# The scan's second block gets a buffer of its own and is prepared among the value streams; the recurrent streams' weights are loaded by single feature tiles

## The chip, the cores and the metric

The kernel runs on one core of a Trainium2 chip. The metric is the device time of one execution in microseconds (us). Five engines work side by side, each through its own instructions in the order in which they are written into the program: PE (matrix products), DVE (vector), ACT (scalar and activation functions), POOL and SP (here mostly the issuer of DMA transfers). They meet through semaphores. An instruction that waits holds up everything behind it on its engine.

## What is computed

One layer of a bidirectional encoder on 1024 tokens of width 1024: a SwiGLU feed-forward block, a mixing layer, a second feed-forward block, each between RMS norms. The mixing layer projects the normed tokens once (`z = h @ w_in`), runs dilated attention on one part of the columns and a bidirectional RWKV-7 recurrence on the other, and projects both back. Of the recurrence this is what matters here:

```python
def _rwkv7_step(state, inp):
    r, w, k, v, kk, kka = inp
    sa = jnp.einsum('dbhvk,dbhk->dbhv', state, kk)
    state = state * w[..., None, :] - sa[..., :, None] * kka[..., None, :] + v[..., :, None] * k[..., None, :]
    y = jnp.einsum('dbhvk,dbhk->dbhv', state, r)
    return state, y
```

r, k and v are columns of z, each token mixed with its two neighbours; kk is k scaled and normalised by head; the decay w and the rate inside kka come from small products of z. There are eight heads of 64 features and two directions.

## The kernel before

**How the work is staged.** First feed-forward block, projection of the attention columns, attention; under the attention the engines already work at the recurrent streams; then the scan; then the output projection and the second feed-forward block. The change lies between the end of attention and the first quarter of the scan.

**The streams.** `project_rwkv` (L499) makes the twelve recurrent streams, one for each feature tile (`ct`) of 128 features: 4 to 7 are k, 0 to 3 are r, 8 to 11 are v (stream 0 is made elsewhere). Its argument is a list of (first tile, number of tiles) pairs. For each pair `columns` (L426) loads eight pieces of the weight, one for each 128 rows, into `zraw` (L431, four buffers) and splits each into a high part `zh` (ACT, L186) and a low part `zl` (DVE, L187); both have sixteen buffers, which is two pairs' worth. Each feature tile is then 48 matrix products of 512 tokens (L510): two halves of the tokens, eight pieces, three products. `shift` mixes in the neighbours (ACT L522 and L523, DVE L524 and L525), and `stream` stores the tile. A value tile is also reversed (DVE L605), turned by PE (L611), copied out by ACT (L613) and stored in token order (SP, L615); the scan reads it back later. I call the four value streams V8 to V11.

**The scan** walks over eight blocks of 128 tokens, each block in both directions. A block goes through four steps:

- `prep` (L783): for each direction, loads of decay, rate, r, k and kk (`in`, `th_w`, `th_a`), two exponentials, six DVE operations (L810, L811, L814, L815, L821, L822), 16 products `lp` (L830) whose results DVE masks into `lm` (L832, four times), and 16 transposes `bp` (L838). One direction is called a half-preparation below. At the end the diagonal pieces of `lm` go to memory (L846).
- `solve` (L850): loads those pieces as `X`, and inverts 32 by 32 triangles in 31 pairs of DVE operations (L866, L868), each of which needs the one before; a copy (L870) ends it; POOL stores the result (L872, L873).
- `merge` (L875): POOL loads the result back (L883, L886), PE makes the 64 by 64 inverses (`pa` L894, `pb` L900), ACT copies them (L896, L902).
- `chain` (L918): two chunks of 64 tokens after each other, each of them xu (L941), a copy `xs` (L944), xu again (L952), a copy `uv` (L954), the new state `st` and the output y (L937), and the state's product with the decay on DVE (L968, twice for a chunk). The next chunk starts from that.

What `prep` leaves of a block (`lm`, `pr`, `bt`, `gc`; 32 KB in each partition) lives until its chain has ended. Before the change block 0 has the buffer `R0`, which is taken from space beside the streams' tiles, and the other blocks have the two buffers of the pool `B0`, which lies where the normed tokens `x` were. So block 1's buffer is free only when the last value product has read x. Blocks 3 and 5 use `R0` again.

**What sets the order.** The program is written in the order of `run` (L1163), and a scheduler places every instruction on its engine by that order as a priority and by its own idea of when inputs are ready. `upto(m)` prepares and solves blocks up to m; `project_attended` (L1066) is the attention half of the output projection of 128 tokens (24 products of 512 columns, L1064, with weights `woh` and `wol` whose low part DVE makes at L1055); it is called twice after chain 0 and once after each later chain.

Of the kernel before, what the change touches and what calls it, by code (L numbers as in the profile page):

```python
# [10 lines left out]
F32 = mybir.dt.float32  # L11
# [152 lines left out]
class _Kernel:  # L164
# [998 lines left out]
    def run(self):  # L1163
        nc = self.nc
        R = dict(side="right")
# [3 lines left out]
        with self.top as top:  # L1169
# [5 lines left out]
            x = self.operand(xp, xp)  # L1175
            x0 = self.io["x"][0]

            with ExitStack() as st:
# [6 lines left out]
                f = self.factors(x, xt)  # L1185
# [50 lines left out]
                x = x2  # L1236
# [10 lines left out]
            s_mc, s_at, s_sc, s_ps = (ExitStack() for _ in range(4))  # L1247
# [11 lines left out]
            NB, s_sr, s_pr, s_zr, s_pm = NC_ // BLK, ExitStack(), ExitStack(), ExitStack(), ExitStack()  # L1259
            pm = self.pool(s_pm, "ps_m", 1, space=PSUM, **R)  # L1260
            pp = self.pool(s_pr, "ps_p", 3, space=PSUM, **R)
            sp = self.pool(s_sr, "prep", 1, **R)
            R0 = self.pool(s_sr, "blk0", 1, **R)
            self.scan_constants(sp)
            zr, pz = self.pool(s_zr, "zr", 2), self.pool(s_zr, "ps_r", 1, space=PSUM)
            self.project_rwkv(zr, pz, x, [(4, 2), (6, 2), (1, 1), (2, 2)])
            blk = {0: self.prep(0, sp, pp, R0)}
            self.solve(0, sp)
            self.project_rwkv(zr, pz, x, [(8, 2), (10, 2)])
            s_zr.close()  # L1270
            s_xn.close()
            B0 = self.pool(s_sc, "blks", 2)
            sc = self.pool(s_sc, "scan")
            self.scan_inverses(sc)
            sc.tile([128, 96], F32, name="edge")
            s_eo, s_pe = ExitStack(), ExitStack()
            eo = self.pool(s_eo, "eo")
            pc = self.pool(s_ps, "ps_c", 1, space=PSUM)
            pe = self.pool(s_pe, "ps_e", 1, space=PSUM)
            self.sv = {}  # L1280
            nxt = [1]

            def upto(m):
                while nxt[0] <= min(m, NB - 1):
                    n = nxt[0]
                    blk[n] = self.prep(n, sp, pp, R0 if n in (3, 5) else B0)
                    self.solve(n, sp)
                    nxt[0] += 1

            upto(1)  # L1290
            rs_a = self.rstd(eo, self.ss_a.rearrange("p a b -> p (a b)"), NT * H, 1.0 / HD, EPS)
            self.merge(0, blk[0], sc, pm)
            upto(2)
            WA = self.out_weights(eo, 0, self.aog)
            for n in range(NB):
                if n:
                    self.merge(n, blk[n], sc, pm)
                self.chain(n, blk.pop(n), sc, pc)
                upto(n + 3)
                for t in ([0, 1] if n == 0 else [n + 1] if n + 1 < NT else []):  # L1300
                    self.project_attended(eo, sc, pe, t, WA, rs_a)
# [5 lines left out]
            x = self.operand(xr, xr, n=4)  # L1307
# [29 lines left out]
            f = self.factors(f0, None)  # L1337
# [97 lines left out]
```

## Time and profile before

| | |
|---|---|
| three runs | 2389.86, 2390.91, 2396.3 us; median 2390.91 |
| the profiled execution | 2398.21 us |
| its span, first to last instruction | 2396.4 us |
| PE, DVE, ACT, POOL busy | 93%, 74%, 43%, 24% |
| mean granted PE clock | 0.951 |

Times in the profile are microseconds from the span's start. A row of the view by engine names start, duration, engine, line and operation, what is written from what, how many follow each other, and in brackets how long the engine had been idle before and which instruction ended the wait. DVE operations that don't depend on each other overlap a little, so two that each last 0.69 us start 0.61 us apart. PE durations overlap too. The windows view gives each engine's busy time in a stretch, with the number of instructions in brackets, the granted PE clock, the DMA engines' busy share and their rate.

### The profile page before, as it was taken

The numbers are of one execution on the slowest core, as the hardware profiler recorded it, in microseconds if no ns is written. First come the engines' busy times: TensorE is split into PE (matmuls) and PEld (weight loads), VectorE is DVE, ScalarE is ACT, GpSimd is POOL, SyncE is SP. The second block draws the span as 40 slices with busy tenths as digits, with TensorE's granted clock in tenths as the row PEclk, the third lists the DMA queues.
The fourth block names the chain that finished last, engine by engine and source line by source line (L and its number), as shares of the span: only waits on it lengthen the run. The fifth ranks groups of instructions, "written<-read, shape, count | busy, mean of one in ns | idle before, by whom it ended". The sixth has DMA issues, their size and how long they took to land. (4 is left out here: it accounts for less than half of the span.)

```text
span 2396.4 us, 39330 instructions
## 1 busy us (share of the span) xinstructions
PE 2233.1 (93%) x14532; PEld 1801.5 (75%) x14532; DVE 1778.9 (74%) x2917; ACT 1030.6 (43%) x1918; POOL 572.8 (24%) x668
## 2 busy tenths in 40 slices
PE   6999999999999998999986788898989999999997
PEld 4788888788786676778775577775768888887886
DVE  8899999865675345666556766746889999997565
ACT  4422333354676304556544444445442233335452
POOL 6244344500000010111101121132234443442000
PEclk8999999999999998999995698789989999999999
DMA  5344544576743415322366766558534544448655
GB/s 155 110 172 150 171 158 156 181 257 194 227 152 133 161 50 157 84 71 72 91 173 174 177 157 166 146 173 268 186 107 172 180 150 167 164 152 268 194 189 180
DMA packets 359763, 386.03 MB, mean 161 GB/s; under 512 B 73618, under 2 KB 268050, under 8 KB 359572
## 3 DMA queue, kind: packets, MB, share of 16 engines
q1 hardware_dynamic: 311968, 284.82, 39.5%
q0 software_dynamic: 27248, 86.05, 9.7%
q10 hardware_dynamic: 20356, 12.66, 1.8%
q8 instruction: 114, 1.87, 0.3%
q14 instruction: 77, 0.63, 0.1%
HBM read 257.53 MB, written 125.89 MB: 160 GB/s over the span
## 5 line engine op out<-in xcount | busy, mean ns | idle before, releaser
L186 ACT ACTIVATE wh<-raw 128x512 fp32r<-128x512 f32 (+1 forms) x273 | 168.2, 627 | 261.8 <-DVE raw L62 94.0
L81 PE MATMUL gu<-xh,wh 128*128 128x512 f32 x704 | 277.2, 394 | 2.3 <-ACT wh L186 1.1
L187 DVE TENSOR_TENSOR wl<-raw,wh 128x512 fp32r<-128x512 f32 (+1 forms) x273 | 275.6, 1013 | 2.1 <-ACT wh L186 1.2
L81 PE MATMUL gu<-xh,wl 128*128 128x512 f32 x704 | 275.9, 392 | 0.0
L81 PE MATMUL gu<-xl,wh 128*128 128x512 f32 x704 | 275.7, 392 | 0.0
L415 PE MATMUL pd<-gl,gwh 128*128 128x512 f32 x616 | 240.5, 390 | 2.5 <-DVE gl L187 2.5
L415 PE MATMUL pd<-gh,gwh 128*128 128x512 f32 x616 | 239.6, 390 | 0.6 <-DVE row L86 0.6
L415 PE MATMUL pd<-gh,gwl 128*128 128x512 f32 x616 | 239.8, 389 | 0.0
L86 DVE TENSOR_TENSOR row<-gu,row 128x512 f32<-128x512 f32 x308 | 206.3, 682 | 26.1 <-PE gu L81 24.2
L187 DVE TENSOR_TENSOR gwl<-graw,gwh 128x512 fp32r<-128x512 f32 (+1 forms) x176 | 117.9, 672 | 128.4 <-ACT gwh L186 125.7
L116 POOL DMA_DIRECT2D d_hid<-row x154 | 84.7, 551 | 473.3 <-DVE row L114 446.2
L186 ACT ACTIVATE gwh<-graw 128x512 fp32r<-128x512 f32 (+1 forms) x176 | 101.4, 576 | 188.4 <-PE pd L415 157.5
L81 PEld LDWEIGHTS gu<-xh,wh 128*128 128x128 f32 x704 | 133.5, 190 | 31.6 <-ACT xh L186 2.0
L81 PEld LDWEIGHTS gu<-xl,wh 128*128 128x128 f32 x704 | 133.4, 189 | 27.5
L81 PEld LDWEIGHTS gu<-xh,wl 128*128 128x128 f32 x704 | 133.1, 189 | 27.6
L415 PEld LDWEIGHTS pd<-gl,gwh 128*128 128x128 f32 x616 | 115.6, 188 | 28.0 <-DVE gl L187 4.3
L415 PEld LDWEIGHTS pd<-gh,gwh 128*128 128x128 f32 x616 | 115.6, 188 | 25.3 <-DVE row L86 1.0
L415 PEld LDWEIGHTS pd<-gh,gwl 128*128 128x128 f32 x616 | 115.7, 188 | 23.8
L187 DVE TENSOR_TENSOR gl<-raw,gh 128x512 fp32r<-128x512 f32 x160 | 112.3, 713 | 17.0 <-ACT gh L186 16.7
L94 ACT ACTIVATE row<-row 128x512 f32<-128x512 f32 x44 | 27.8, 633 | 221.3 <-DVE row L86 217.5
L145 POOL TENSOR_TENSOR ws<-ws 128x512 f32<-128x512 f32 x88 | 114.2, 1298 | 1.1
L186 ACT ACTIVATE gh<-raw 128x512 fp32r<-128x512 f32 x160 | 98.0, 621 | 33.7 <-DMA raw<-in_ffn_w_down_dram 21.8
(354 smaller groups left out, 5345.7 us busy)
## 6 DMA issues: line engine op xcount, KB each, us to landing
d_hid<-row POOLq DMA_DIRECT2D x154, 256.0 KB, 2.4
graw<-d_hid SPq DMA_DIRECT2D x132, 256.0 KB, 3.0
raw<-in_ffn_w_gate_dram SPq DMA_DIRECT2D x88, 256.0 KB, 3.0
raw<-in_ffn_w_up_dram SPq DMA_DIRECT2D x88, 256.0 KB, 3.3
ws<-in_ffn_w_down_dram SPq DMA_DIRECT2D x88, 256.0 KB, 4.5
d_ws<-ws POOLq DMA_DIRECT2D x88, 256.0 KB, 2.3
raw<-d_ws SPq DMA_DIRECT2D x88, 256.0 KB, 2.7
raw<-in_ffn_w_down_dram SPq DMA_DIRECT2D x66, 256.0 KB, 3.6
```

The lines of the kernel that those rows point to most:

```text
L81: self.K.nc.tensor.matmul(ps, a[:, k, :], b[:, k, :], start=(k == 0 and i == 0), stop=(k == 3 and i == 2))
L86: add = lambda o, x: V.tensor_tensor(o, ps, x, op=OP.add)
L94: A.activation(y[:, 0], y[:, 0], AF.Silu)
L116: put = lambda n, y: G.dma_start(self.hid[n - 1, j // 2], y)
L145: G.tensor_tensor(o, a, b, op=OP.subtract)
L186: self.nc.scalar.activation(h, src, AF.Copy)
L187: (eng or self.nc.vector).tensor_tensor(l, src, h, op=OP.subtract)
L415: T.matmul(ps[x], a[:, ts], b, start=(m == 0 and k == 0), stop=(m == NM - 1 and k == 2))
```

## The change

The streams' weights come by single tiles in place of pairs, so `zh`, `zl` and `zraw` have half the size, there are 88 pieces in place of 48, and the sixteen buffers hold two feature tiles in place of up to four. The space goes to `R1`, a second buffer beside `R0`. Block 1 is prepared into it and solved between V9 and V10 in the program's text. `B0` keeps one buffer, for blocks 2 and 6; blocks 4 and 7 take `R1` (before, 1, 2, 4, 6 and 7 took turns in the two of `B0`). Which earlier block has to end before a block can be prepared is thereby the same as before for all blocks but 1. The `edge` tile only keeps the next pool at a multiple of 128 bytes.

```diff
-            R0 = self.pool(s_sr, "blk0", 1, **R)
+            R0, R1 = (self.pool(s_sr, f"blk{j}", 1, **R) for j in range(2))
...
-            self.project_rwkv(zr, pz, x, [(4, 2), (6, 2), (1, 1), (2, 2)])
-            blk = {0: self.prep(0, sp, pp, R0)}
-            self.solve(0, sp)
-            self.project_rwkv(zr, pz, x, [(8, 2), (10, 2)])
+            self.project_rwkv(zr, pz, x, [(ct, 1) for ct in (4, 5, 6, 7, 1, 2, 3)])
+            blk = {}
+            for n, ct in ((0, 8), (1, 10)):
+                blk[n] = self.prep(n, sp, pp, (R0, R1)[n])
+                self.solve(n, sp)
+                self.project_rwkv(zr, pz, x, [(ct, 1), (ct + 1, 1)])
...
-            B0 = self.pool(s_sc, "blks", 2)
+            B0 = self.pool(s_sc, "blks", 1)
...
-            sc.tile([128, 96], F32, name="edge")
+            sc.tile([128, 112], F32, name="edge")
...
-            nxt = [1]
+            nxt = [2]
...
-                    blk[n] = self.prep(n, sp, pp, R0 if n in (3, 5) else B0)
+                    blk[n] = self.prep(n, sp, pp, {3: R0, 4: R1, 5: R0, 7: R1}.get(n, B0))
...
-            upto(1)
```

How the scheduler places it is seen at three places.

On DVE, before the change, at the end of block 0's solve (`Ti` is the inverse in the making, `X` its source). The first operations of block 1 that write into its buffer come behind the solve:

```order
L866 TENSOR_TENSOR ttmp<-X,Ti 128x16
L868 TENSOR_TENSOR Ti<-Ti,ttmp 128x16
L870 COPY X<-Ti 128x512
L808 COPY gc<-e_10186 128x8
L810 TENSOR_TENSOR pr<-in_11649,e_10186 128x8x64
L811 TENSOR_TENSOR pr<-in_11649,e_10186 128x8x64
```

On DVE now, at the start of block 0's solve. Its first step comes behind the whole first half-preparation of block 1 and V9's reversal:

```order
L605 COPY vrev<-us 128x1024
L810 TENSOR_TENSOR pr<-in_11579,e_10189 128x8x64
L811 TENSOR_TENSOR pr<-in_11579,e_10189 128x8x64
L814 SCALAR_TENSOR_TENSOR bk<-th_a,in_11579 128x8x64
L187 TENSOR_TENSOR zl<-zraw,zh 128x128
L815 SCALAR_TENSOR_TENSOR bk<-bk,th_w 128x8x64
L187 TENSOR_TENSOR zl<-zraw,zh 128x128
L821 TENSOR_TENSOR th_a<-th_a,in_11579 128x512
L822 TENSOR_TENSOR bk<-th_a,th_w 128x8x64
L832 TENSOR_TENSOR lm<-lp,k_tri 128x512 x4
L866 TENSOR_TENSOR ttmp<-X,Ti 128x31
```

Block 1's first half moved from behind block 0's solve to ahead of it. Within the solve now stand V10's and V11's shifts, four splits, block 1's second half-preparation and the six operations of block 2's first.

On DVE, before, where the first chunk's state of chain 0 is made (L968); block 1's solve begins behind it:

```order
L814 SCALAR_TENSOR_TENSOR bk<-th_a,in_12015 128x8x64
L968 TENSOR_TENSOR sv<-st,gc 64x2x256
L815 SCALAR_TENSOR_TENSOR bk<-bk,th_w 128x8x64
L968 TENSOR_TENSOR sv<-st,gc 64x2x256
L866 TENSOR_TENSOR ttmp<-X,Ti 128x31
L821 TENSOR_TENSOR th_a<-th_a,in_12015 128x512
```

On DVE now, at the same place; block 1's solve has ended (the copy L870), and both chunks' states stand behind it:

```order
L868 TENSOR_TENSOR Ti<-Ti,ttmp 128x16
L870 COPY X<-Ti 128x512
L814 SCALAR_TENSOR_TENSOR bk<-th_a,in_12648 128x8x64
L1055 SCALAR_TENSOR_TENSOR wol<-wor,c_attn_out_g,woh 128x512
L815 SCALAR_TENSOR_TENSOR bk<-bk,th_w 128x8x64
L968 TENSOR_TENSOR sv<-st,gc 64x2x256 x2
```

Block 1's solve moved from behind chain 0's first state to ahead of it.

On PE, before, at merge 1 (`pa`), which stands behind both half-preparations of block 3 and 24 products of `project_attended` (`po`):

```order
L830 MATMUL lp<-pr,bk 128x128 x16
L838 MATMUL bp<-ident,bk 128x64 x8
...
L1064 MATMUL po<-woh,yal 128x512
L894 MATMUL pa<-d_12704,lm 32x32
L1075 MATMUL yq<-ident,yat 128x128 x4
L894 MATMUL pa<-d_12704,lm 32x32 x31
L941 MATMUL xu<-sv,lm 64x64
L1064 MATMUL po<-woh,yah 128x512
```

On PE now, from the end of chain 0's second chunk to the first product of chain 1:

```order
L937 MATMUL y<-lm,uv 64x64 x15
L830 MATMUL lp<-pr,bk 128x128 x16
L838 MATMUL bp<-ident,bk 128x64 x8
L894 MATMUL pa<-d_12947,lm 32x32
L937 MATMUL st<-sv,ident 64x256
L894 MATMUL pa<-d_12947,lm 32x32 x11
...
L900 MATMUL pb<-tt_12090,d_12947 32x32 x31
L941 MATMUL xu<-sv,lm 64x64
L1075 MATMUL yq<-ident,yat 128x128 x4
L830 MATMUL lp<-pr,bk 128x128 x16
L838 MATMUL bp<-ident,bk 128x64 x8
L1064 MATMUL po<-woh,yah 128x512
```

Merge 1 moved ahead of block 3's second half-preparation and of all those products; this half-preparation and all 48 products of the two calls now stand between merge 1 and the first state of chain 1. From block 3's solve on, both orders are nearly the same up to the last blocks.

## The prediction, on record before the run

> **What bounds the kernel now.** I read the busy times in stretches first, chosen so that each holds one state of affairs: attention with the streams under it, the value streams, the start of the scan, a hole in it, the rest.
>
> ```profile
> 900.00:1205.00 305.00, 292.95 (x2655) 235.26 (x2655) 188.13 (x511) 170.60 (x371) 40.01 (x45) 0.95 0.34 97
> 1205.00:1260.00 55.00, 46.86 (x278) 36.85 (x276) 35.89 (x75) 25.46 (x47) 2.13 (x3) 0.97 0.67 173
> 1260.00:1340.00 80.00, 59.64 (x721) 51.61 (x722) 51.36 (x122) 38.32 (x70) 10.29 (x16) 0.62 0.66 173
> 1340.00:1360.00 20.00, 4.21 (x30) 2.81 (x32) 19.40 (x84) 6.55 (x12) 5.78 (x10) 0.59 0.70 161
> 1360.00:1420.00 60.00, 54.71 (x742) 43.12 (x739) 40.42 (x120) 28.17 (x51) 13.03 (x21) 0.85 0.63 165
> 1420.00:1625.00 205.00, 181.69 (x3124) 148.36 (x3122) 124.26 (x362) 94.05 (x177) 43.24 (x62) 0.87 0.63 167
> ```
>
> The columns are length, then busy PE, PE's weight loads, DVE, ACT, POOL, the granted PE clock and the DMA. Until 1205 PE bounds (293 of 305 us). From 1260 to 1360 nothing is full over the whole stretch: PE works 64 of 100 us at a clock of about 0.6, and from 1340 DVE is full while PE stands. There is room of some 36 us and a slow clock. Who waits for whom is told by the timeline of DVE, with the copy L870 as the end of a solve and L968 as the making of a state:
>
> ```profile
> 1226.75 1.29 DVE L832 TENSOR_TENSOR lm<-lp,k_tri 128x512 f32<-128x512 f32 x2 [0.44 <-PE lp L830]
> ...
> 1235.77 0.69 DVE L822 TENSOR_TENSOR bk<-th_a,th_w 128x512 f32<-128x512 f32 x1
> 1243.74 1.28 DVE L524 SCALAR_TENSOR_TENSOR us<-u,c_rwkv_mu_prev,us 128x1023 f32<-128x1023 f32 x1 [7.29 <-ACT us L523]
> 1244.95 0.18 DVE L866 TENSOR_TENSOR ttmp<-X,Ti 128x31 f32<-128x31 f32 x1
> ...
> 1267.54 0.60 DVE L870 COPY X<-Ti 128x512 f32<-128x512 f32 x1
> ...
> 1313.36 0.68 DVE L968 TENSOR_TENSOR sv<-st,gc 64x512 f32<-64x512 f32 x1
> 1313.96 0.67 DVE L815 SCALAR_TENSOR_TENSOR bk<-bk,th_w 128x512 f32<-128x512 f32 x1
> ...
> 1330.74 0.68 DVE L968 TENSOR_TENSOR sv<-st,gc 64x512 f32<-64x512 f32 x1 [0.49 <-PE st L937]
> ...
> 1352.12 0.58 DVE L870 COPY X<-Ti 128x512 f32<-128x512 f32 x1
> ...
> 1374.32 0.62 DVE L870 COPY X<-Ti 128x512 f32<-128x512 f32 x1
> ...
> 1391.85 0.68 DVE L968 TENSOR_TENSOR sv<-st,gc 64x512 f32<-64x512 f32 x1
> ...
> 1401.35 0.68 DVE L968 TENSOR_TENSOR sv<-st,gc 64x512 f32<-64x512 f32 x1 [0.29 <-PE st L937]
> ...
> 1414.85 0.60 DVE L870 COPY X<-Ti 128x512 f32<-128x512 f32 x1
> ...
> 1428.27 1.41 DVE L968 TENSOR_TENSOR sv<-st,gc 64x512 f32<-64x512 f32 x2 [1.07 <-PE st L937]
> ```
>
> Solve 0 ends at 1268, but solve 1 only at 1352, 84 us later, because block 1 could not be prepared until x was released. Chain 0 has its second state at 1331; chain 1 has its first at 1392. The 61 us between hang on solve 1. PE's side of it, and chain 0's end on ACT:
>
> ```profile
> 1269.46 4.79 PE L830 MATMUL lp<-pr,bk 64*128 64x128 f32 x29 [2.03 <-DVE pr L811]
> ...
> 1282.73 0.31 PE L894 MATMUL pa<-d,lm 32*32 32x32 f32 x2 [7.66 <-DMA d<-d_t]
> ...
> 1334.15 2.05 PE L830 MATMUL lp<-pr,bk 64*128 64x128 f32 x24
> ...
> 1354.84 0.79 PE L1064 MATMUL po<-woh,yah 128*128 128x512 f32 x1 [13.87 <-ACT woh L1054]
> ...
> 1379.67 0.39 PE L1064 MATMUL po<-woh,yal 128*128 128x512 f32 x1
> 1379.90 0.40 PE L1064 MATMUL po<-woh,yah 128*128 128x512 f32 x1
> ```
> ```profile
> 1331.67 0.65 ACT L970 COPY yb<-y 128x256 f32<-128x256 f32 x2 [0.27 <-PE y L937]
> ```
>
> The largest hole, 13.87 us, is put down to the weights of the output projection. Those wait for their low parts on DVE, which stand behind the steps of two solves.
>
> **The change part by part.** First the small edits. Single tiles need 88 splits in place of 48:
>
> ```profile
> L187 DVE TENSOR_TENSOR zl<-zraw,zh 128x256 fp32r<-128x256 f32 x40 | 16.7, 430 | 6.1 <-ACT zh L186 5.6 <-PE zr L510 0.2
> L186 ACT ACTIVATE zh<-zraw 128x256 fp32r<-128x256 f32 x40 | 15.8, 414 | 8.2 <-PE zr L510 6.0 <-DMA zraw<-in_w_in_dram 2.1
> ```
> ```profile
> L186 ACT ACTIVATE zh<-zraw x48: 299/416/430, 923.3 to 1193.3; 128x256 fp32r<-128x256 f32 x40, 128x128 fp32r<-128x128 f32 x8
> L187 DVE TENSOR_TENSOR zl<-zraw,zh x48: 228/419/834, 932.6 to 1194.7; 128x256 fp32r<-128x256 f32 x40, 128x128 fp32r<-128x128 f32 x8
> ```
> ```profile
> zraw<-in_w_in_dram SPq DMA_DIRECT2D x40, 128.0 KB, 2.5
> zraw<-in_w_in_dram SPq DMA_DIRECT2D x8, 64.0 KB, 2.7
> ```
>
> The shortest of 48 (299 and 228 ns) are the eight of single width. So 40 wide ones become 80 narrow ones: ACT 80 x 0.299 - 15.8 = +8.1 us, DVE 80 x 0.228 - 16.7 = +1.5 us. ACT is busy 171 and DVE 188 of the 305 us in which PE is full, so PE hides both; without it they would cost up to 10 us. Half the bytes land no sooner (2.7 against 2.5 us). A tile's eight pieces go through four buffers in two rounds of about 2.7 + 0.3 + 0.23 + 0.3 for the issue = 3.5 us, 7 us in all, while its 48 products take 48 x 0.23 = 11 us: covered, with 4 us to spare. I take nothing; the bound is 4 us for each of the last three tiles, if four more us get lost in each. The 40 more issues on SP's queue stand where it has time, but for the last four of V11, which now queue behind the stores of block 0's pieces and behind the reload of X.
>
> Now the move. Two DVE prices go into it:
>
> ```profile
> 1255.34 0.29 DVE L866 TENSOR_TENSOR ttmp<-X,Ti 128x128 f32<-128x128 f32 x1
> 1255.66 0.29 DVE L868 TENSOR_TENSOR Ti<-Ti,ttmp 128x128 f32<-128x128 f32 x1
> ...
> 1336.88 0.28 DVE L866 TENSOR_TENSOR ttmp<-X,Ti 128x126 f32<-128x126 f32 x1
> 1337.08 0.75 DVE L1055 SCALAR_TENSOR_TENSOR wol<-wor,c_attn_out_g,woh 128x512 fp32r<-128x512 f32 x1
> 1337.74 0.28 DVE L868 TENSOR_TENSOR Ti<-Ti,ttmp 128x126 f32<-128x126 f32 x1
> ```
>
> A large step of a solve takes 0.32 us when it follows the one it needs, and 0.20 us with other work between. An ordinary operation takes 0.6 us (1313.36 to 1313.96). So a half-preparation is 10 x 0.61 = 6.1 us of DVE.
>
> Step 1, solve 0 begins. Ahead of block 0's last masking stand seven more value products on PE (1.6 us) and one shift on DVE (1.2): 1228.0 becomes 1231, and the solve's start, 17 us behind it through memory, 1245 becomes 1247.5. Block 1's first half-preparation falls into the hole of 7.29 us: free.
>
> Step 2, solve 0 ends. It took 23.2 us. Into it come the second half-preparation (6.1), six operations of block 2 (3.6), more of V10's shift (1.2) and four splits (0.9): +11.8. Some 35 steps now have a neighbour: -35 x 0.12 = -4.2. Twice DVE has to wait for PE, which stands at V11's products, whose splits are in this very solve; no row shows it, I bound it by 0 and the 10 us in which PE's order has nothing else, and take 6, near the 7.29 us of the like wait above. So 36.8 us, and the end moves from 1268 to 1284. That is 16 us **later**.
>
> Step 3, chain 0. Merge 0 begins 14.6 us after its solve (1268.1 to 1282.7): 1299. Until the first state it took 30.6 us with some two half-preparations on PE; now one, for which block 2's operations come at about 1307: 26 us, 1325 in place of 1313. The second chunk, free of half-preparations, takes 9.5 us (1391.85 to 1401.35) in place of 17.4: 1334.5 in place of 1330.7. Its last reads of `R0` are queued behind block 3's first products and part of merge 1 on PE: 1342 in place of 1333.
>
> Step 4, solve 1. After 1284 DVE has 62 steps (about 16 us), a half-preparation and a masking (8.5), weights (2.7) and waits for PE's `lp` behind merge 0 (9): 1320 in place of 1352, 32 us **earlier**. Merge 1 could start at 1335.
>
> Step 5, chain 1's first state. Now PE's order decides: block 3's second half-preparation and 48 products stand ahead of it, and block 3 needs `R0`. From 1342: 10.5 us of DVE (masks, operations, two weights, steps between), 4 to 7 us of `lp` and `bp` (the rows at 1334 and 1269), 48 x 0.23 = 11 us, and 11 us of merge, xu, copies and st: 1381 in place of 1392. That is the gain: 11 us. The 13.87 us hole is gone, and what is late next is block 3 behind chain 0.
>
> Step 6. From there the orders agree and every wait hangs on the one before, so 10 us stay to the end. Near it, chain 5's first state now comes behind 42 steps of the last solve in place of 9; 33 x 0.3 = 10 us later, though the last solve then ends sooner by about as much as it was held up. I take 0, bounds -6 to +10.
>
> Sum: 2398.2 us of the profiled execution less 10. It lies 7.3 us above the median of the runs, so for the median I subtract the same: 2390.9 - 10 = **2381 us**. Its own range is 2369 to 2388: 6 us less by step 2 and 6 by step 6, or 4 more by step 2 and a part of the 10 of step 6, the whole of which is rival C.
>
> **The rivals.** A measurement can tell about 0.3% here, 7 us.
>
> A, far faster: merge 1 is ready at 1335, and if PE is not held up by block 3, the first state of chain 1 comes at about 1350 to 1360. Gain 30 to 40 us, 2356. For it: solve 1 is 32 us early, and PE has 36 us of room. Against it: PE's order.
>
> B, slower, in chain 0: the clock. PE now stands from about 1290 to 1299 for merge 0, as it did for 7.66 us before, and after that the row shows 0.62 over 80 us. My chain 0 and block 3 hold some 45 us of PE work at near full clock. From a chain 0 that ends at 1353, 11 us later than I have it, the gain of step 5 is used up. If two thirds of that work run at 0.62, it takes 30 x 0.61 = 18 us longer; with the upper bound of step 2 (4 more) the end is at 1364, 11 us past that point: 2402. All of it at 0.62 would give 2412. [...]
>
> C, no change: the 10 us are given back by chain 5 (step 6) or by later waits for memory: 2391.
>
> D, the single tiles starve PE: 4 us for each of three tiles, which delay all behind them: 2381 + 12 = 2393. Against it: 4 us to spare in each tile.
>
> That the block isn't prepared earlier can be left out: the order shows it.
>
> **The numbers.** My forecast 0.43, A 0.13, C 0.20, B 0.20, D 0.04. A lies under 2383.7 (0.3% faster), and so does most of the forecast (0.37): faster 0.50. Same: C, D and 0.06 of the forecast, less a little of C and D that goes past 2398: 0.29. Slower: B and that little, 0.21. The range takes in the forecast, C, D, the near half of A and B's likelier price: 2360 to 2403.
>
> **What would show it.** In the profile after: solve 0's L870 at about 1284, solve 1's at 1320, chain 0's states at 1325 and 1335, chain 1's first at 1381; no wait of PE for `woh` over 5 us; PE waiting about 9 us for `pa`; about 293 us of PE until 1205. I am wrong if solve 0 ends by 1275, if chain 1 is not held by block 3, or if the lead at chain 1 is not found at 1625.

## The result, and the profile after

The changed kernel takes 2376.85 us (median of nine, 2369.55 to 2383.48), the kernel before 2392.15 us in the same comparison: a ratio of 0.9934, with a 95% interval of 0.9917 to 0.9951. That is 15.3 us less, where the forecast was 10 less. The profiled execution took 2381.76 us with a span of 2379.6 us, 5 us above its median, as the one before was 6 to 7 above its own.

The stretches of the prediction, now in the changed kernel (length, then busy PE, weight loads, DVE, ACT, POOL, the granted PE clock, the DMA share):

```profile
900.00:1205.00 305.00, 292.92 (x2670) 235.11 (x2669) 191.67 (x544) 171.97 (x398) 40.20 (x46) 0.96 0.33 93
...
1260.00:1340.00 80.00, 54.17 (x700) 46.18 (x700) 59.90 (x172) 39.48 (x72) 18.02 (x29) 0.67 0.82 198
1340.00:1360.00 20.00, 20.00 (x233) 16.69 (x228) 13.79 (x36) 13.96 (x26) 0.00 (x0) 0.71 0.61 166
...
1420.00:1625.00 205.00, 171.31 (x2908) 138.09 (x2904) 128.43 (x370) 96.52 (x182) 43.93 (x59) 0.90 0.66 179
```

Until 1205 nothing has changed (292.92 against 292.95 us of PE). From 1340 to 1360, where PE stood for 16 of 20 us, it is now full. That the last stretch is emptier only says that the scan ends sooner within it. DVE's timeline in the changed kernel shows the same marks as before, L870 for the end of a solve and L968 for the making of a state:

```profile
1237.61 0.69 DVE L810 TENSOR_TENSOR pr<-in,e 128x512 f32<-128x512 f32 x1 [1.42 <-DMA in<-d_rk]
...
1248.01 0.18 DVE L866 TENSOR_TENSOR ttmp<-X,Ti 128x31 f32<-128x31 f32 x1
...
1279.86 0.59 DVE L870 COPY X<-Ti 128x512 f32<-128x512 f32 x1
...
1315.00 0.60 DVE L870 COPY X<-Ti 128x512 f32<-128x512 f32 x1
1319.30 1.41 DVE L968 TENSOR_TENSOR sv<-st,gc 64x512 f32<-64x512 f32 x2 [0.68 <-PE st L937]
...
1326.41 1.39 DVE L968 TENSOR_TENSOR sv<-st,gc 64x512 f32<-64x512 f32 x2
...
1332.69 0.19 DVE L866 TENSOR_TENSOR ttmp<-X,Ti 128x31 f32<-128x31 f32 x1 [4.68 <-DMA X<-d_x]
...
1371.30 0.60 DVE L870 COPY X<-Ti 128x512 f32<-128x512 f32 x1
...
1372.95 0.68 DVE L968 TENSOR_TENSOR sv<-st,gc 64x512 f32<-64x512 f32 x1
```

Block 1's first half-preparation (from the row at 1237.61 on) stands where the old hole of 7.29 us was. Solve 0 ends 12 us later than before, solve 1 37 us earlier, and chain 1's first state 19 us earlier. PE's timeline:

```profile
1296.11 0.31 PE L894 MATMUL pa<-d,lm 32*32 32x32 f32 x2 [8.46 <-DMA d<-d_t]
...
1326.19 1.10 PE L937 MATMUL y<-lm,uv 128*64 128x64 f32 x29
1327.22 2.05 PE L830 MATMUL lp<-pr,bk 64*128 64x128 f32 x24
1334.43 1.43 PE L830 MATMUL lp<-pr,bk 64*128 64x128 f32 x5 [5.16 <-DVE lm L832]
...
1387.88 0.31 PE L894 MATMUL pa<-d,lm 32*32 32x32 f32 x2
```

The 13.87 us wait for `woh` is gone, the wait for `pa` is still there, and the largest new one is 5.16 us, for a mask of block 3 on DVE. That mask stands behind the first steps of block 2's solve, and these wait 4.68 us for their `X` (DVE's row at 1332.69). The last row is the start of merge 2.

**One clock for all traces.** Executions of one kernel differ by some 10 us or more, and part of that lies ahead of the change. Attention ends with the last sum of L737, which the rows of the view by line give as the end of their range, first before, then after:

```profile
L737 DVE TENSOR_REDUCE ss_a<-far x8: 687/687/691, 971.4 to 1173.8; 128x8 f32<-128x512 f32 x8
```
```profile
L737 DVE TENSOR_REDUCE ss_a<-far x8: 687/689/689, 977.6 to 1178.4; 128x8 f32<-128x512 f32 x8
```

The changed kernel's profiled execution reached that point 4.6 us later. So below, marks of the scan are counted in us from the end of attention: chain 1's first state comes at 218.0 before and at 194.5 after, and chain 7's last copy of y at 449.9 and 428.3. Every mark is the start of its row; the mark of a solve is the start of the copy that ends it.

### The profile page after: what moved, and what is told of

It reads as the page before. It is cut to its first block, busy times and chain, and to the rows that moved or that the text cites. A ratio compares the mean times of both kernels' runs of the same rounds, so it can differ in the third digit from the quotient of the medians.

```text
span 2379.6 us, 39492 instructions
## 1 busy us (share of the span) xinstructions
PE 2215.2 (93%) x14532; PEld 1789.4 (75%) x14532; DVE 1781.9 (75%) x2957; ACT 1034.2 (43%) x1958; POOL 568.9 (24%) x668
## 4 chain that ended last, share of the span: by engine, by line
PE 38%; DVE 6%; DMA 6%; ACT 2%; issue 2%; SPq 1%; POOL 1%; DVEq 0%; POOLq 0%; ACTq 0%
PE gu L81 17%; PE pd L415 9%; PE zr L510 2%; PE po L1064 1%; DMA in<-d_rk 1%; PE lp L830 1%; PE po L707 1%; DVE Ti L868 1%; PE st L937 1%; DVE ttmp L866 1%; PE pt L700 1%; DMA wor<-in_w_out_dram 1%; PE y L937 1%; DMA d_vt<-vts 0%; DMA d<-d_t 0%
## 5 line engine op out<-in xcount | busy, mean ns | idle before, releaser
L81 PE MATMUL gu<-xl,wh 128*128 128x512 f32 x704 | 275.6, 391 | 0.0
L187 DVE TENSOR_TENSOR gwl<-graw,gwh 128x512 fp32r<-128x512 f32 (+1 forms) x176 | 118.1, 673 | 131.9 <-ACT gwh L186 128.0
```

The source lines that it names most:

```text
L81: self.K.nc.tensor.matmul(ps, a[:, k, :], b[:, k, :], start=(k == 0 and i == 0), stop=(k == 3 and i == 2))
L187: (eng or self.nc.vector).tensor_tensor(l, src, h, op=OP.subtract)
```

## The experiments

Each time is a median; the ratio is to the kernel before on the same chip, with a 95% interval. The table that collects the marks stands behind the last experiment.

**Single tiles alone.** The kernel before with only the lists changed:

```diff
-            self.project_rwkv(zr, pz, x, [(4, 2), (6, 2), (1, 1), (2, 2)])
+            self.project_rwkv(zr, pz, x, [(ct, 1) for ct in (4, 5, 6, 7, 1, 2, 3)])
...
-            self.project_rwkv(zr, pz, x, [(8, 2), (10, 2)])
+            self.project_rwkv(zr, pz, x, [(ct, 1) for ct in (8, 9, 10, 11)])
```

> The kernel before, with the streams' weights by single tiles and nothing else: one block buffer R0, block 1 prepared when x is released. Theory 1 (the gain is block 1's early preparation in a buffer of its own): no gain, 0 to +4 us against the kernel before, block 0's pr (L810) about 6 us later because its loads stand behind more weight loads on SP, solve 1 ends near 1352 to 1358, chain 1's first state (L968) at 1390 to 1398, the long wait of PE for woh still there. Theory 2 (the single tiles themselves bring it, by finer loads and copies): -10 to -15 us, chain 1's first state at about 1375.

Measured: 2389.84 us, ratio 0.9995 (0.9983 to 1.0008). The tiles bring nothing and cost nothing, so theory 2 is out. Of the marks that theory 1 expected, the wait for `woh` is still there (13.21 us), but block 0's `pr` comes at 31.5 us from the end of attention, where it came at 30.8 before: 0.7 us later and not 6. This kernel is also the better picture of "before": it has the same time, and its profiled execution lies near its median. The end of attention, and its rows on DVE, on PE (the start of merge 2) and on ACT:

```profile
L737 DVE TENSOR_REDUCE ss_a<-far x8: 687/689/689, 972.0 to 1170.6; 128x8 f32<-128x512 f32 x8
```
```profile
1342.81 0.58 DVE L870 COPY X<-Ti 128x512 f32<-128x512 f32 x1
...
1364.32 0.61 DVE L870 COPY X<-Ti 128x512 f32<-128x512 f32 x1
...
1381.50 0.68 DVE L968 TENSOR_TENSOR sv<-st,gc 64x512 f32<-64x512 f32 x1 [0.22 <-PE st L937]
...
1418.81 1.41 DVE L968 TENSOR_TENSOR sv<-st,gc 64x512 f32<-64x512 f32 x2 [2.44 <-PE st L937]
...
1454.57 1.39 DVE L968 TENSOR_TENSOR sv<-st,gc 64x512 f32<-64x512 f32 x2 [2.63 <-PE st L937]
```
```profile
1397.23 1.20 PE L894 MATMUL pa<-d,lm 32*32 32x32 f32 x64
```
```profile
1613.16 0.65 ACT L970 COPY yb<-y 128x256 f32<-128x256 f32 x2 [2.17 <-PE y L937]
```

From 1170.6, solve 1 ends at 172.2, the first states of chains 1 and 2 come at 210.9 and 248.2, chain 3's second state at 284.0 and the last y at 442.6. The 449.9 us of the profile of before are 7 us more, though the times are the same, so I take these 7 us to be that execution's own.

**The buffer, but late in the text.**

```diff
-            for n, ct in ((0, 8), (1, 10)):
-                blk[n] = self.prep(n, sp, pp, (R0, R1)[n])
-                self.solve(n, sp)
-                self.project_rwkv(zr, pz, x, [(ct, 1), (ct + 1, 1)])
+            blk[0] = self.prep(0, sp, pp, R0)
+            self.solve(0, sp)
+            self.project_rwkv(zr, pz, x, [(ct, 1) for ct in (8, 9, 10, 11)])
+            blk[1] = self.prep(1, sp, pp, R1)
+            self.solve(1, sp)
```

> The changed kernel, R1 kept, but block 1's preparation and solve written behind all four value streams, as late in the text as in the kernel before. Theory 1a (the buffer alone is enough, the scheduler fills the holes): solve 1 still ends well before chain 1 is wanted, chain 1's first state within 4 us of the changed kernel's 1373, -12 to -16 us. Theory 1b (it needs the place among the value streams too): solve 1's steps mix with chain 0 as in the kernel before and end at about 1340, chain 1's first state at 1380 to 1388, -3 to -9 us.

Measured: 2392.49 us, ratio 0.9999 (0.9986 to 1.0012). Not even the 3 to 9 us of theory 1b. On DVE:

```profile
1272.42 0.59 DVE L870 COPY X<-Ti 128x512 f32<-128x512 f32 x1
...
1335.09 0.58 DVE L870 COPY X<-Ti 128x512 f32<-128x512 f32 x1
...
1381.19 0.68 DVE L968 TENSOR_TENSOR sv<-st,gc 64x512 f32<-64x512 f32 x1 [1.48 <-PE st L937]
```

Solve 1 ends 63 us behind solve 0, where in the changed kernel 35 us lie between them. A free buffer isn't used by itself: the place in the text decides when its work is done. PE has no wait for `woh` in this run; a wait of 8.74 us for `yat` (DVE, L1072) has come near its place.

**The products of `project_attended` later, in the kernel before.**

```diff
-                for t in ([0, 1] if n == 0 else [n + 1] if n + 1 < NT else []):
+                for t in ([] if n == 0 else [0, 1, 2] if n == 1 else [n + 1] if n + 1 < NT else []):
```

> The kernel before, with the two calls of project_attended that follow chain 0 moved behind chain 1 in the text; no buffer added. Theory 3 (the gain is that the wait for woh, 13.87 us, and the products in front of merge 1 go, whatever block 1 does): -8 to -15 us, chain 1's first state at about 1378. Theory 1: PE has nothing to do there anyway until solve 1 has ended at 1352, merge 1 is limited by it, chain 1's first state 1380 to 1390, and the products come back later: -5 to +3 us in all.

Measured: 2391.71 us, ratio 1.0002 (0.9988 to 1.0015). The edit does less than it says, since the scheduler still places part of these products in front of merge 1, and a wait of 12.72 us for `woh` remains. So this run doesn't try theory 3. What speaks against it is the run with the late buffer: there the wait for `woh` is gone, and nothing was gained.

**Chain 1 ahead of block 3, in the changed kernel.**

```diff
-                upto(n + 3)
+                upto(n + 3 if n else 2)
```

> The changed kernel, with block 3's preparation written behind chain 1 in place of chain 0 (from block 4 on the order is as it was). My step 5 (chain 1 is held by block 3 and the 48 products): chain 1's first state comes 15 to 25 us earlier, at 1348 to 1358, but solve 3 ends later than 1408, and chain 3 gives it back: -3 to +8 us against the changed kernel. Rival A's price (a chain 1 not held by block 3 is worth 20 us more to the end): 15 to 20 us under the changed kernel. If chain 1's first state does not move by more than 5 us, step 5 named the wrong holder.

Measured: 2397.54 us, ratio 1.0037 (1.0021 to 1.0054), some 20 us over the changed kernel. On DVE, chain 1's first state, the end of solve 3 and chain 3's second state:

```profile
1347.34 0.68 DVE L968 TENSOR_TENSOR sv<-st,gc 64x512 f32<-64x512 f32 x1 [0.35 <-PE st L937]
...
1423.84 0.58 DVE L870 COPY X<-Ti 128x512 f32<-128x512 f32 x1
...
1469.99 0.68 DVE L968 TENSOR_TENSOR sv<-st,gc 64x512 f32<-64x512 f32 x1 [2.82 <-PE st L937]
```

Attention ended at 1175.5 here. Block 3 did hold chain 1 (step 5): without it, the state comes 21 to 23 us earlier than in the changed kernel's two profiles. But rival A's price was wrong in sign, at least when chain 1 is freed in this way. Block 3's solve ends 19 to 25 us later, chain 3 waits for it, and more is lost there than was gained. My expectation (at most +8) was too mild.

**The same products later, in the changed kernel.** The edit is the one shown for these products in the kernel before.

> The changed kernel with the two calls of project_attended that follow chain 0 moved behind chain 1 in the text; block 3 stays where it is. Step 5 (the 48 products are a part of what holds chain 1): chain 1's first state (L968) 8 to 12 us earlier than 1373, solve 3 still at about 1408, and since the second run showed solve 3 to have room, the end 5 to 11 us earlier: 2366 to 2372. Rival (chain 1's date is worth nothing as long as block 3's solve ends at the same time, or the products come back in front of merge 2): 0 to +5 us against the changed kernel.

Measured: 2388.81 us, ratio 0.9974 (0.9956 to 0.9991), some 10 us over the changed kernel. The forecast for the mark held: from the end of attention, chain 1's first state comes at 181.6 in place of 192.4 to 194.5. The forecast for the end failed by more than the rival had it: of the 72 products that now follow chain 1, PE's timeline has 24 ahead of the end of merge 2 and the others amid chain 2.

**Chain 1 between the halves of block 3.** `prep` calls merge 1 and chain 1 at its half:

```diff
-    def prep(self, n, p, psum, big):
+    def prep(self, n, p, psum, big, amid=None):
...
         for d in range(2):
+            if d and amid:
+                amid()
```

> The changed kernel with merge 1 and chain 1 written between the two half-preparations of block 3, the middle between the changed kernel and the run with chain 1 ahead of all of block 3. Theory: the end is set by the later of two strands, chain after chain (chain 1's date) and block after block (solve 3's date); the changed kernel is held by the first, chain 1 ahead of block 3 by the second. Then the middle gains: chain 1's first state 12 to 20 us earlier than 1373, solve 3 at 1410 to 1425 in place of 1408, the end 4 to 10 us earlier than the changed kernel. Rival (block 3's date alone sets the end): as much later as solve 3 comes later, +3 to +10 us.

Measured: 2385.60 us, ratio 0.9968 (0.9949 to 0.9988): 8 us over the changed kernel, in the rival's range. Chain 1's first state comes 20 us earlier, but chain 2's comes 3 to 9 us later. The theory that the middle gains falls.

**Eight raw buffers.** In the profile after, block 0's preparation seemed late: SP's queue stood at weight loads until 1204, first the changed kernel, then this run.

```profile
1182.15 21.68 SPq L182 DMA_DIRECT2D zraw<-in_w_in_dram  x17
1204.13 0.38 SPq L182 DMA_DIRECT2D in<-d_rk  x1
```
```profile
1183.85 21.38 SPq L182 DMA_DIRECT2D zraw<-in_w_in_dram  x17
1205.58 0.38 SPq L182 DMA_DIRECT2D in<-d_rk  x1
```

```diff
-            hl = self.columns(p, ATT + c0 * 128, n * 128)
+            hl = self.columns(p, ATT + c0 * 128, n * 128, bufs=8)
```

> The changed kernel with eight buffers for the raw pieces of a stream's weight in place of four. If the loads of block 0's preparation came 6 us late because SP's queue stood behind weight loads that waited for a buffer: block 0's pr (L810) at about 1205 in place of 1211, solve 0 and chain 0 some 5 us earlier, the end 3 to 6 us earlier than the changed kernel. If the lateness was taken up later (chain 1 does not hang on chain 0's start): pr earlier and the end within 2 us.

Measured: 2391.91 us, ratio 0.9994 (0.9975 to 1.0014): the whole gain is lost. The theory falls: with twice the buffers the same 17 loads still take 21 us, and `pr` comes at 1210.70, as in the changed kernel (1210.71). And the lateness was that of one execution: from the end of attention, block 0's `pr` comes 30.8 us behind in the kernel before and 32.3 us after. Where this run loses its 15 us isn't settled. Its profiled execution is the shortest of its twelve, and shows solve 1 ending 10 us and the last y 3 us later than the changed kernel's first.

**Block 1 one value stream earlier, and one later.**

```diff
-            for n, ct in ((0, 8), (1, 10)):
+            for n, cts in ((0, (8,)), (1, (9, 10, 11))):
                 blk[n] = self.prep(n, sp, pp, (R0, R1)[n])
                 self.solve(n, sp)
-                self.project_rwkv(zr, pz, x, [(ct, 1), (ct + 1, 1)])
+                self.project_rwkv(zr, pz, x, [(ct, 1) for ct in cts])
```

> The changed kernel with block 1 prepared and solved behind V8 in the text, one value stream earlier. If the gain comes from DVE work of block 1 put under the value products, wherever it stands there: solve 1 ends 3 to 8 us earlier, chain 1's first state within 5 us of 1373, the end within 4 us of the changed kernel. If block 1's work delays solve 0 and with it chain 0 (my step 2, 12 us): solve 0 ends 3 to 8 us later than 1280 and the end comes as much later. The rival that block 1 is best prepared as early as can be: 5 us or more under the changed kernel.

Measured behind V8: 2383.23 us, ratio 0.9951 (0.9929 to 0.9972). For the later place the list is `((0, (8, 9, 10)), (1, (11,)))`.

> The changed kernel with block 1 prepared and solved behind V10 in the text, one value stream later. Of this place two neighbours are measured: behind V8 the time was 12 us and behind V11 no us under the kernel before, behind V9 (the changed kernel) 13 to 16. If chain 1 is held by PE's order (block 3 and the 48 products stand in front of it) and not by solve 1 itself, solve 1 may end 5 us later without harm, and solve 0, freed of a part of block 1, ends earlier: within 4 us of the changed kernel, -11 to -18 against the kernel before. If the gain falls with every value product that no longer covers block 1: halfway between V9 and V11, -5 to -9.

Measured behind V10: 2382.86 us, ratio 0.9963 (0.9948 to 0.9978). So behind V8, V9, V10 and V11 block 1 is worth about 10 to 12, 13 to 16, 8 to 9 and 0 us. Behind V8, solve 0 ends 2 to 3 us later and chain 0's first state comes 8 to 11 us later than in the changed kernel, in the direction of step 2. Behind V10, solve 1 ends 3 to 6 us later, and the time lies in the range of that run's rival, not in mine. That the earliest place is the best, by 5 us or more, is out. Behind V11 the gain is gone, which is clear of the intervals. The order of V8, V9 and V10 is not: the interval behind V8 overlaps both others widely, and V10's reaches into V9's (0.9934 and, below, 0.9947), so that the gain falls with every value product that no longer covers block 1 is not shown.

**The changed kernel again.**

> The changed kernel itself, beside the next two on the same chip, as the measure for them and for the variants before, which lay 6 to 15 us above it. Expected: 2374 to 2380 us, -12 to -18 against the kernel before. If it comes out above 2383, the first measurement was lucky and the variants with a later product or eight raw buffers cost less than they seemed.

Measured: 2376.53 us, ratio 0.9947 (0.9931 to 0.9963), so the gain stands. This second profile is near its median. Its rows:

```profile
L737 DVE TENSOR_REDUCE ss_a<-far x8: 687/689/690, 969.4 to 1172.1; 128x8 f32<-128x512 f32 x8
```
```profile
1306.20 0.61 DVE L870 COPY X<-Ti 128x512 f32<-128x512 f32 x1
...
1364.49 0.68 DVE L968 TENSOR_TENSOR sv<-st,gc 64x512 f32<-64x512 f32 x1
...
1402.67 1.41 DVE L968 TENSOR_TENSOR sv<-st,gc 64x512 f32<-64x512 f32 x2 [2.94 <-PE st L937]
...
1432.17 0.69 DVE L810 TENSOR_TENSOR pr<-in,e 128x512 f32<-128x512 f32 x1 [2.45 <-PE y L937]
...
1436.29 1.39 DVE L968 TENSOR_TENSOR sv<-st,gc 64x512 f32<-64x512 f32 x2 [2.82 <-PE st L937]
...
1504.82 0.59 DVE L870 COPY X<-Ti 128x512 f32<-128x512 f32 x1
...
1544.49 0.68 DVE L968 TENSOR_TENSOR sv<-st,gc 64x512 f32<-64x512 f32 x1 [2.54 <-PE st L937]
```
```profile
1596.22 0.65 ACT L970 COPY yb<-y 128x256 f32<-128x256 f32 x2 [2.17 <-PE y L937]
```

From 1172.1, solve 1 ends at 134.1, the first states of chains 1 and 2 come at 192.4 and 230.6, chain 3's second at 264.2, the last y at 424.1. Against the single tiles alone that is 38, 18.5, 17.6, 19.8 and 18.5 us earlier. The row at 1432.17 shows what comes next: block 5's first product waits for a `y` of chain 3, because block 5 takes block 3's buffer.

**The buffers in rotation, in the changed kernel and in the kernel before.** Block 5 takes the pool's buffer, free since chain 2, and block 6 takes `R0`:

```diff
-                    blk[n] = self.prep(n, sp, pp, {3: R0, 4: R1, 5: R0, 7: R1}.get(n, B0))
+                    blk[n] = self.prep(n, sp, pp, {3: R0, 4: R1, 6: R0, 7: R1}.get(n, B0))
```

> The changed kernel with the block buffers in strict rotation: block 5 takes the pool's buffer (free when chain 2 has ended), block 6 takes R0 (free when chain 3 has ended); before, block 5 takes R0 and block 6 the pool's buffer. Theory of two strands: from chain 3 on the end is held by block 5, which cannot be prepared before chain 3 has ended (chain 3's last state 1448, solve 5 ends 1516, chain 5's first state 1555). With the rotation block 5 starts at about 1430, solve 5 ends at 1485 to 1500, chain 5's first state at 1520 to 1535, and if nothing else takes over the end is 10 to 25 us earlier. Rival: DVE is full there (the same work, only earlier, delays chain 3 and 4 by as much): within 4 us of the changed kernel.

Measured: 2366.25 us, ratio 0.9895 (0.9876 to 0.9913), 10 us under the changed kernel beside it. It is the shortest time of this study. On DVE, block 5's first product, chain 3's second state, the end of solve 5 and chain 5's first state, and the last y on ACT:

```profile
1407.47 0.68 DVE L810 TENSOR_TENSOR pr<-in,e 128x512 f32<-128x512 f32 x1
...
1452.58 0.68 DVE L968 TENSOR_TENSOR sv<-st,gc 64x512 f32<-64x512 f32 x1
...
1485.39 0.61 DVE L870 COPY X<-Ti 128x512 f32<-128x512 f32 x1
...
1520.81 1.41 DVE L968 TENSOR_TENSOR sv<-st,gc 64x512 f32<-64x512 f32 x2 [2.90 <-PE st L937]
```
```profile
1589.31 0.65 ACT L970 COPY yb<-y 128x256 f32<-128x256 f32 x2 [2.17 <-PE y L937]
```

Attention ended at 1168.2 here. Counted from it and against the second profile of the changed kernel, block 5 starts 21 us earlier and chain 5's first state comes 20 us earlier, as expected. Chain 3 pays 20 us for it, since block 5's work now stands ahead of it, but block 5 no longer waits for chain 3. The last y comes 3 us earlier than in that profile and 7 us earlier than in the first; by the times it is 10, the lower end of what was expected. So of the 20 us at chain 5 the larger part is lost again behind it. The same two timelines show where: solves 6 and 7 end only 1 and 3 us earlier than in that profile.

> The kernel before with the same rotation (block 5 in the buffer of block 2, block 6 in R0 after block 3). If the lead that block 1's buffer gives and the hold by block 5 are independent terms, the rotation brings the same here as in the changed kernel. If the lead of the changed kernel is what makes block 5 the late one, it brings less than half of that here.

In the kernel before the same rotation (`R0 if n in (3, 6) else B0`) gives 2382.89 us, ratio 0.9967 (0.9950 to 0.9983): 9 us by the medians, 8 by the ratio, where the changed kernel gained 10 by the medians. The intervals allow some 4 us either way, so the two terms add up as far as this can tell.

**The marks of all runs**, in us from the end of attention, from each run's own rows. Time is the median less that of the kernel before beside it.

| kernel | solve 1 ends | chain 1, first state | solve 3 ends | chain 2, first state | chain 3, second state | last y less the mark before it | time |
|---|---|---|---|---|---|---|---|
| kernel before | 178.3 | 218.0 | 241.1 | 254.5 | 290.6 | 159.3 | 0 |
| single tiles alone | 172.2 | 210.9 | 233.8 | 248.2 | 284.0 | 158.6 | -1.8 |
| buffer late | 161.8 | 207.9 | 226.2 | 246.2 | 283.2 | 160.0 | +0.9 |
| products late, before | 172.1 | 207.4 | 241.3 | 249.8 | 281.7 | 159.8 | +0.1 |
| changed, first profile | 136.6 | 194.5 | 229.6 | 236.7 | 270.1 | 158.2 | -15.3 |
| changed, second profile | 134.1 | 192.4 | 223.6 | 230.6 | 264.2 | 159.9 | -15.4 |
| products late, changed | 134.3 | 181.6 | 225.9 | 237.3 | 275.6 | 159.2 | -4.3 |
| chain 1 amid block 3 | 134.0 | 172.4 | 242.4 | 239.5 | 284.6 | 153.9 | -7.5 |
| chain 1 ahead of block 3 | 136.4 | 171.8 | 248.3 | 233.0 | 294.5 | 151.2 | +6.0 |
| block 1 behind V8 | 131.9 | 196.8 | 230.5 | 238.4 | 270.7 | 162.3 | -9.9 |
| block 1 behind V10 | 139.7 | 199.0 | 228.2 | 235.2 | 269.1 | 158.8 | -8.2 |
| eight raw buffers | 146.8 | 197.8 | 228.2 | 235.8 | 270.1 | 161.3 | -1.2 |
| rotation, before | 174.7 | 214.9 | 236.8 | 251.2 | 294.5 | 136.6 | -9.0 |
| rotation, changed | 132.3 | 193.5 | 225.3 | 232.5 | 284.4 | 136.7 | -25.6 |

Two things are to be seen. As long as block 5 uses block 3's buffer, the last y comes 158 to 162 us behind chain 3's second state, whatever was done ahead of it (151 and 154 where block 3 was put off). With the rotation it is 137, but that is no gain of 22 us: in the changed kernel 20 of them are chain 3's own lateness. And chain 2's first state follows chain 1's by 36 to 42 us where chain 1 comes at 192 or later; where chain 1 comes at 172 to 182, chain 2 still waits until 233 to 240. The rows of merge 2 show both sides of this. It starts 7 us behind chain 1's second state in the single tiles alone (1397.23 against 1389.94) as in the changed kernel (1387.88 against 1380.51), so chain 1's lead is handed on. But solve 2, which merge 2 needs as well, ends only 1 to 3 us earlier in the changed kernel: merge 2 starts 32 us behind its end in the one (1364.93) and 16 us in the other (1371.90). With block 1 behind V8, PE already waits 1.34 us there for what solve 2 has stored, 13.6 us behind its end. So the changed kernel has used up all but some 2 us of what an earlier chain 1 alone can bring at merge 2. Single executions scatter by several us (the two profiles of the changed kernel differ by 6 at chain 3), so smaller differences in the table aren't to be read. The eight raw buffers don't fit: by their marks they should be some 10 us under the single tiles alone, and by their time they are level with them.

## Why the prediction was right, and where it was not

**The small edits: right.** PE's 292.92 us until 1205 and the single tiles alone (0.9995) leave nothing for rival D.

**Step 1: near.** Solve 0 began at 1248.01 (forecast 1247.5), and block 1's first half was free. That the two figures agree so well is luck: counted from the end of attention it is 69.6 where the forecast amounts to 73.7, and 71.1 before.

**Step 2: the direction right, one term wrong.** I added 6 us in which DVE waits for PE inside solve 0. The stretch of that solve in the changed kernel:

```profile
1248.01:1280.46 32.45, 25.02 (x149) 19.32 (x148) 30.91 (x93) 18.02 (x36) 1.09 (x3) 0.94 0.79 209
```

DVE is busy for 30.91 of 32.45 us, so there was hardly any such wait. Without it my sum is 30.8 us.

**Step 3: the step that failed most.** I had chain 0's last reads of `R0` at 1342, behind block 3's first products and part of merge 1. In the trace they are the `y` products that end at 1327.3, and block 3's `lp` follows right behind them. The products of L937 that do stand amid merge 1, from 1336 to 1345, are the first of chain 1, which read `R1`. The merge came 15.6 us behind the solve, as taken (14.6), but from there the first state took 23 us (I had 26) and the second 7.1 (I had 9.5).

**Step 4: right in kind.** Solve 1 ended at 1315.60 (1320): 37 us earlier than before.

**Step 5: the holder right, the size too small.** Chain 1 was held by what I named. Moving the 48 products brings its first state forward by 11 to 13 us, moving block 3 by 21 to 23. It came at 1372.95 (1381); against the single tiles alone it was 16 to 18.5 us earlier where I had 11. The path behind step 3 took 45.6 us from 1327.3, not my 39; the wait of block 2's solve for `X` (4.68 us, and PE's 5.16 us behind it) is in it, and I had put no such wait there. So one term was 15 us too late and the next 6.6 us too short, and that the sum came out as near as it did is in part luck.

**Step 6: the sum right, the reason only half.** That every wait hangs on the one before holds from chain 1 to chain 3 and on to the end, but only for a chain 1 as late as 192. Any earlier, and chain 2 is held by merge 2: solve 2 leaves it some 2 us, and in the three runs that went further it was held up or drawn out by what PE had still to do for block 3 or for the products. I named chain 5's lateness and took 0 for it, and 158.6 against 158.2 and 159.9 us from chain 3's second state to the last y bear this out.

**The rivals.** A's mechanism, a chain 1 that block 3 does not hold, was made true by two runs, and cost 8 and 21 us against the changed kernel. B did not come: the clock from 1260 to 1340 was 0.67, not lower than 0.62. C failed, since the lead of chain 1 was found at the end.

What stays open: why eight raw buffers lose the gain. That the late place of block 1 loses by solve 1's later end is what the marks suggest, but block 2's and block 3's work moved with it and was not tried apart; with the buffer late, solve 1 ended 10 us earlier than in the single tiles alone, and the time was the same. What takes back most of the rotation's 20 us at chain 5 was followed no further than to solves 6 and 7.

## What to carry over

A buffer of its own lets work start early only if the program's order puts that work where its engine has room: here the same buffer was worth 0 to 15 us by its place alone. Before pricing an earlier date for one link of a chain, look for the date from which the next link is held by something else; here three variants brought chain 1 forward by 11 to 23 us more, and all three ended later. When the distance from one mark to the end is the same in many variants, look for a buffer that may make it so, and then at the end and not at the mark: the rotation, a change of one table, brought chain 5 forward by 20 us and the end by 10.

## What the hardware showed

In the changed kernel the granted clock fell from 1.00 (1274 to 1276) to 0.50 (from 1277 on), just behind a wait of PE of 4.20 us that ended at 1275.80. PE then stood for 8.46 us until 1296, and again for 3.23 us until 1300, with the clock at 0.50 all the while. The stretches behind that show how long it stayed there (0.50 in all of them but the last two):

```profile
1300.00:1304.00 4.00, 3.34 (x44) 3.09 (x42) 2.65 (x9) 1.21 (x2) 0.00 (x0) 0.50 0.82 196
1304.00:1308.00 4.00, 4.00 (x77) 3.71 (x76) 2.00 (x5) 2.37 (x4) 0.00 (x0) 0.50 0.80 214
1308.00:1312.00 4.00, 4.00 (x62) 3.49 (x63) 2.51 (x7) 3.22 (x5) 0.00 (x0) 0.50 0.87 244
1312.00:1316.00 4.00, 4.00 (x69) 3.53 (x65) 3.55 (x15) 2.87 (x5) 0.73 (x1) 0.50 0.42 74
1316.00:1320.00 4.00, 3.32 (x54) 3.21 (x56) 2.23 (x4) 3.58 (x7) 2.46 (x4) 0.50 0.71 156
1320.00:1324.00 4.00, 4.00 (x98) 3.62 (x96) 2.08 (x3) 2.28 (x6) 2.91 (x7) 0.88 0.19 43
1324.00:1328.00 4.00, 4.00 (x107) 3.73 (x104) 3.50 (x6) 1.78 (x4) 1.68 (x3) 1.00 0.87 213
```

From 1300 to 1320 PE is busy for 18.7 of 20 us, with small products (writing 32 to 128 columns each), and the clock stays at 0.50; from 1320 to 1321 it is 0.54, from 1321 to 1322 it is 1.00. So in this trace it came back only after some 20 us of nearly unbroken work. In the kernel before it went to 0.50 at 1262, behind a wait of PE of 4.07 us that ended at 1261.02, was 0.50 until 1308 and, after 1.00 from 1312 to 1316, 0.50 to 0.52 from 1316 to 1328. Rival B's mechanism, a half clock over a good part of chain 0, thus was there, in the kernel before as in the changed one; what failed was that it should grow. It did not begin with the wait for merge 0, as B had it: in both kernels the clock was at 0.50 before that wait (7.66 and 8.46 us) began. What keeps the clock down, and what ends it, was not tried.
